# Other start addresses for the operands of both feed-forwards of a two-layer hybrid trunk

## The chip, the cores and the metric

The kernel runs on one core of a Trainium2 chip. The metric is the device time of one launch in microseconds (us), lower is better.

## What is computed

The reference is a trunk of two layers on a sequence of 256 positions with 2048 features, in float32. Layer 0 is differential attention and a gated feed-forward with a causal depthwise convolution (ConvFFN); layer 1 is a gated DeltaNet and another ConvFFN. Each of the four parts works on an RMS-normed copy of x and is added to x. The change touches the two feed-forwards:

```python
def conv_ffn(h, w_up, conv_w, conv_b, w_down):
    u = causal_dwconv(h @ w_up, conv_w) + conv_b
    val, gate = jnp.split(u, 2, axis=-1)
    return (jax.nn.silu(gate) * val) @ w_down

for i in range(DEPTH):
    h = rms_norm(x, mixer_norm[i])
    ...
    x = x + conv_ffn(rms_norm(x, ffn_norm[i]), ffn_w_up[i], ffn_conv_w[i], ffn_conv_b[i], ffn_w_down[i])
```

D_FF is 5504, which is 43 tiles of 128 to each half of w_up.

## The kernel before, in words

Activations lie transposed: features on the 128 partitions, the 256 positions along the free axis. Each float32 operand of a projection is split in two parts, hi (rounded to the type fp32r) and lo (what is left), and a product is made of three matmuls: hi times hi, lo of the weights times hi, hi of the weights times lo (lines 115, 116 and 117). Each matmul loads 128 columns of weights into the array (the stationary operand) and lets 256 columns of activations stream through (the moving operand); in the profile the load is a LDWEIGHTS of its own, on PEld, and overlaps the matmul ahead of it.

Each projection goes through `dense` (line 101), which makes one block of 256 output features: for each chunk of 4 tiles of the contraction, `weights` (line 78) brings the raw weights by a DMA of 512 KB from SyncE's queue, ScalarE casts them to `whi` (line 89), VectorE subtracts to get `wlo` (line 90), and TensorE does 4 x 2 x 3 = 24 matmuls. Raw, whi and wlo have three buffers each. `dense_tok` (line 125) is the other way round: the activations are stationary and the weights moving (line 139); attention's v and DeltaNet's z use it.

A feed-forward (`ffn`, line 251) makes 43 up-blocks (16 contraction tiles each, acts in `h`) with merge, convolution, SiLU and `split` behind each, which leaves one tile row of `ac` (lines 218, 219), and then `project` (line 238) makes 8 down-blocks (43 contraction tiles each, acts in `ac`). When a block of the down-projection has been added to x, the callback `done` writes the next part's normed tiles into `h` (`norm_tile`, lines 152 and 153). Attention's output projection and DeltaNet's do the same for the feed-forward behind them. DeltaNet's output blocks read their acts from tiles `oc`. The order of the work on each engine is the order of the program's lines; small jobs of attention and DeltaNet are fed in between chunks by `tick`.

Where the operands begin is set by hand. Addresses are counted in words of 4 bytes along a partition, modulo 128 words (512 bytes). All rows, chunks and column groups of a tile stand a multiple of 128 words apart, so that one number holds for a whole tile: the first word of `h` is at 40 (HP), of `ac` at 48 (AP; attention's own tiles `ac` too), of `oc` at 112 (OP); the whi and wlo buffers begin at 0 and have 128 words of room, and `weights` puts the block `d` words into them. `dense` takes `d = (place - GAP) % P` with GAP = 45: the weights of every block begin 45 words (180 bytes) ahead of the acts that stream against them. `dense_tok` takes `(HP + GAP) % P` = 85, so that there as well the moving operand stands 45 words behind the stationary one. `rows` cuts a tile of acts in rows that begin `d` words in, and `place(d)` does so for `h`; the kernel before has `d` = 0 in both. `h` and `ac` are allocated with 8 words to spare.

Of the kernel before, what the change touches and what calls it, by code (L numbers as in the profile page):

```python
# [9 lines left out]
F32R = mybir.dt.float32r  # L10
# [6 lines left out]
P = 128  # L17
T = 256
D = 2048
KD = D // P  # L20
EPS = 1e-6
CK = 4
GAP = 45
HP, AP, OP = 40, 48, 112
LNEXP = "natural_log_exp_and_others"

# [1 line left out]
class Trunk:  # L28
# [38 lines left out]
    def mp(self):  # L67
        return self.mps.tile([P, 512], F32, tag="mp", name="mp")
# [29 lines left out]
    def banks(self):  # L98
        return self.dps.tile([P, 2, 2 * T], F32, tag="ps", name="ps")

    def dense(self, w, kt, acts, place, tiles=2, lead=0):

        nc = self.nc
        ps = self.banks()
        for k0, nk in self.chunks(kt, CK, lead):
            hi, lo = self.weights(w[:, k0:k0 + nk, :], (place - GAP) % P)
            steps = [(k, c) for k in range(nk) for c in range(tiles)]
            if k0 + nk == kt:
                steps = [(k, c) for c in range(tiles) for k in range(nk)]
            for k, c in steps:  # L110
                a = acts(k0 + k)
                first, last = k0 + k == 0, k0 + k == kt - 1
                s = slice(c * P, (c + 1) * P)
                o = ps[:, c, :T]
                nc.tensor.matmul(o, hi[:, k, s], a[:, 0, :], start=first, stop=False)  # L115
                nc.tensor.matmul(o, lo[:, k, s], a[:, 0, :], start=False, stop=False)  # L116
                nc.tensor.matmul(o, hi[:, k, s], a[:, 1, :], start=False, stop=last)  # L117
            self.tick()
        return ps
# [5 lines left out]
    def dense_tok(self, w, kt, acts):  # L125
# [3 lines left out]
        for k0, nk in self.chunks(kt, CK // 2):  # L129
            hi, lo = self.weights(w[:, k0:k0 + nk, :], (HP + GAP) % P)  # L130
            for k in range(nk):
# [103 lines left out]
                done(2 * blk + c)  # L235
            self.add_squares()

    def project(self, w, kt, acts, place, done, final=False):

        n = KD // 2  # L240
        for b in range(n):
            ps = self.dense(w[b], kt, acts, place)
            if b < n - final:
                self.add_out(b, ps, done)
                continue
            for c in range(2):
                k = 2 * b + c
                self.nc.vector.tensor_tensor(self.x[:, k, :], ps[:, c, :T], self.x[:, k, :], ALU.add)
                done(k)

    def ffn(self, w_up, w_down, nj, cols_ap, done, final=False):

        nc = self.nc
        self.spawn(self.norm_stat())
        with self.tc.tile_pool(name="fp", bufs=1) as fp:
            cols = fp.tile([P, 8 * nj + 64], F32, tag="fcols", name="fcols")[:, :8 * nj]
            cols = cols.rearrange("p (t h j) -> p t h j", t=4, h=2)
            nc.scalar.dma_start(cols, cols_ap)
            acts = []
            rows = self.rows(fp.tile([P, nj * 2 * T + 8], F32R, tag="ac", name="ac"), nj, 0)  # L260
            for j in range(nj):
                ps = self.dense(w_up[j], KD, self.h_acts, HP)
                c = []
                u = fp.tile([P, 2, T], F32, tag="u", name="u", bufs=2)
                self.merge(ps, u)
                for half in range(2):
                    o = fp.tile([P, T], F32, tag=f"cv{half}", name="cv", bufs=2)
                    c4 = [cols[:, t, half, j:j + 1] for t in range(4)]
                    self.conv(o, u[:, half, :], c4[:3], c4[3])
                    c.append(o)  # L270
                nc.scalar.activation(c[1], c[1], AF.Silu)
                a = c[0]
                nc.vector.tensor_tensor(a, c[0], c[1], ALU.mult)
                ac = rows[j]
                self.split(ac, a)
                acts.append(ac)
            self.project(w_down, nj, lambda k: acts[k], AP, done, final)

    def attention(self, w_qk, w_v, w_o, nh, dist_ap, ident_ap, qg, kg, lvec, sub, start, done, lambda_init):

        nc, mp = self.nc, self.mp
        with self.tc.tile_pool(name="at", bufs=1) as at:
# [27 lines left out]
            def squares(r):  # L310
                sq = at.tile([P, 2, T], F32, tag="sq", name="sq", bufs=2)
                nc.scalar.square(sq, r)
                sp = at.tile([P, 2, 2, T], F32R, tag="sqp", name="sqp", bufs=3)
                self.split(sp, sq)
                return sp
# [51 lines left out]
            def values(h, v, aT):  # L367
                yield
                po = mp()
                for e in range(2):  # L370
                    o = po[:, e * T:(e + 1) * T]
                    es = slice(e * P, (e + 1) * P)
                    nc.tensor.matmul(o, v[:, 0, es], aT[:, :T], start=True, stop=False)
                    nc.tensor.matmul(o[:, P:], v[:, 1, es], aT[:, T:], start=False, stop=True)
                sq = squares(po.rearrange("p (e t) -> p e t", e=2))
                yield
                pn = mp()
                self.total(pn[:, :T], [sq[:, :, e, :] for e in range(2)])
                ri = at.tile([P, 2, T], F32, tag="ri", name="ori", bufs=2)
                self.rsqrt(ri[:, 0, :], pn[:, :T], 2 * P)  # L380
                for e in range(2):
                    on = at.tile([P, T], F32, tag="on", name="on", bufs=2)
                    nc.vector.scalar_tensor_tensor(
                        on, po[:, e * T:(e + 1) * T], subs[:, e:e + 1], ri[:, 0, :], ALU.mult, ALU.mult)
                    ac = at.tile([P, 2, T], F32R, tag=f"ac{h}_{e}", name="ac")
                    self.split(ac, on)
                    outs.append(ac)

            aTs = []
            for h in range(nh):  # L390
                acts, lead = (self.h_acts, 0) if h else (start, 1)
# [6 lines left out]
            for h in range(0, nh, 2):  # L398
                pv = self.dense_tok(w_v[h // 2], KD, self.h_acts)
                v = at.tile([P, 2, 2 * T], F32, tag="v", name="v", bufs=2)  # L400
                for c in range(2):
                    nc.scalar.mul(v[:, c, :], pv[:, c, :], self.rstdc[:, c:c + 1])
                for i in range(2):
                    self.spawn(values(h + i, v[:, :, i * T:(i + 1) * T], aTs[h + i]))
            self.project(w_o, 2 * nh, lambda k: self.await_(outs, k), AP, done)

    def await_(self, items, k):
# [4 lines left out]
    def gdn(self, w_gate, w_in, w_z, w_out, nb, hb, gate_ap, const_ap, hot_ap, conv_col, ng, done):  # L412
# [12 lines left out]
        with tc.tile_pool(name="gd", bufs=1) as gd:  # L425
# [234 lines left out]
                    acts += [oc[:, i] for i in range(2)]  # L660

            def out(b, acts):
                for blk in range(KD // 2):
                    ps = self.dense(w_out[b * (KD // 2) + blk], 2 * hb, lambda k: self.await_(acts, k), OP)
                    self.add_out(blk, ps, done if b == nb - 1 else None)
# [4 lines left out]
            for b in range(nb):  # L670
# [3 lines left out]
                lqs, inv, acts, zts, vts = [], [], [], {}, {}  # L674
                groups = [range(i, i + gh) for i in range(0, hb, gh)]
                plan = [("k", i) for i in range(hb)] + [("v", 0)] + [("z", g) for g in range(len(groups))]
                for op, i in plan + [("v", i) for i in range(1, hb)]:
# [6 lines left out]
                    elif op == "z":  # L684
                        gr = groups[i]
                        zt = zts[i] = gd.tile([P, 2, gv, P], F32, tag="vz", name="zt", bufs=4)
                        ps = self.dense_tok(w_z[heads[gr[0]] // 2], KD, self.h_acts)
# [14 lines left out]
                if pend:  # L702
                    out(*pend)
                pend = (b, acts)
            out(*pend)

    def gates(self, gd, pg, nv, gp, ident, triu, res):
# [133 lines left out]
def trunk_kernel(tc, a, out):  # L841
    nc = tc.nc
    with ExitStack() as ctx:
# [30 lines left out]
        def start(k):  # L874

            if len(begun) <= k:
                if k == 0 or k in starts:
                    load()
                if k == KD - 1:
# [4 lines left out]
            return t.h[k]  # L884

        t.attention(a["w_qk"], a["w_v"], a["w_o"], NH, a["dist"], a["const"][:, :P], qg, kg, lvec, sub, start, then(ffn, 0),
                    0.8 - 0.6 * math.exp(-0.3 * 0))
        t.ffn(a["w_up0"], a["w_down0"], NJ, a["fcols0"], then(mixer, 1))
        t.gdn(a["w_gate"], a["w_in"], a["w_z"], a["w_out"], NB, HB, a["gate"], a["const"], a["hot"],
              lambda tap, tile_: one(gconv, tap * 4 * NQ + tile_), ng, then(ffn, 1))  # L890
        t.ffn(a["w_up1"], a["w_down1"], NJ, a["fcols1"],
              lambda k: nc.sync.dma_start(out[:, k, :], t.x[:, k, :]), final=True)
# [15 lines left out]
```

## Time and profile before

| what | value |
| --- | --- |
| median of the runs | 2675.66 us (2675.52 and 2675.80) |
| the profiled execution, its own time | 2676.33 us |
| its span, first to last instruction | 2674.6 us |
| granted TensorE clock, mean | 0.999 |
| matmuls and weight loads in the trace | 23504 and 23504 |
| first feed-forward, up and down | about 405 to 874 and 874 to 1108 us |
| second feed-forward, up and down | about 1968 to 2437 and 2437 to 2675 us |

A row of a group reads: line, engine, operation, output<-inputs, shapes, xcount | busy us, mean ns of one | idle time of the engine ahead of them and what ended it. A row of a timeline reads: start in us, duration in us, engine, line, operation; neighbours of one kind can be merged into one row with their count. Matmuls overlap in the records, so the pace of TensorE is read from the distance between starts, or from a stretch's length over its count of matmuls, not from the duration of one. In the tables by windows, a count holds a matmul or two that only reach into the window.

### The profile page before, as it was taken

How to read it: one execution, taken by the hardware profiler on the slowest of the kernel's cores; microseconds unless marked ns; L12 is line 12 of the kernel's file. 1: busy time of each engine (PE TensorE's matmuls, PEld its weight loads, DVE VectorE, ACT ScalarE, POOL GpSimd, SP SyncE). 2: the span in 40 equal slices, each digit the busy share in tenths (PEclk: the TensorE clock that was granted, in tenths of full speed). 3: DMA queues.
4: the chain of work that ended last, by engine and by line, in shares of the span. 5: the costliest groups of instructions: out<-in, count | busy, mean ns of one | idle time of the engine just before them, and what ended most of it. 6: DMA issues, size and time to landing. Idle time of an engine off the chain costs nothing.

```text
span 2674.6 us, 55978 instructions
## 1 busy us (share of the span) xinstructions
PE 2656.4 (99%) x23504; PEld 2639.4 (99%) x23504; DVE 1845.2 (69%) x2719; ACT 1453.3 (54%) x1994; POOL 112.1 (4%) x221
## 2 busy tenths in 40 slices
PE   8999999999999999999999999999999999999999
PEld 8999999999999999999999999999999999999999
DVE  7775567777777555688787687688677777776444
ACT  6555555555555444584764664574565555554333
POOL 0000000000000000031011021021000000000000
PEclk9999999999999999999999999999999999999999
DMA  6555566666666666655355454555466666666765
GB/s 205 172 174 164 159 192 194 195 195 193 195 193 195 193 194 192 190 156 177 115 170 166 143 169 155 157 159 174 143 194 195 194 193 196 193 195 197 203 200 165
DMA packets 135469, 481.77 MB, mean 180 GB/s; under 512 B 15408, under 2 KB 18480, under 8 KB 135216
## 3 DMA queue, kind: packets, MB, share of 16 engines
q1 hardware_dynamic: 134064, 475.58, 58.6%
q8 instruction: 184, 3.01, 0.5%
q10 hardware_dynamic: 1152, 2.61, 0.3%
q14 instruction: 69, 0.57, 0.1%
HBM read 476.03 MB, written 2.10 MB: 179 GB/s over the span
## 4 chain that ended last, share of the span: by engine, by line
PE 93%; DVE 3%; ACT 3%; issue 1%; DMA 1%; ACTq 0%; DVEq 0%; SPq 0%
PE ps L115 26%; PE ps L116 26%; PE ps L117 26%; PE ps L139 10%; PE mp L610 2%; DVE wlo L90 1%; ACT whi L89 1%; PE mp L226 1%; DVE cv L207 1%; ACT L455 0%; PE mp L574 0%; PE mp L580 0%; DMA raw<-w_in 0%; PE mp L589 0%; PE mp L498 0%
## 5 line engine op out<-in xcount | busy, mean ns | idle before, releaser
L90 DVE TENSOR_TENSOR wlo<-raw,whi 128x1024 fp32r<-128x1024 f32 (+2 forms) x909 | 1105.2, 1217 | 660.9 <-ACT whi L89 659.8
L89 ACT CAST whi<-raw 128x1024 fp32r<-128x1024 f32 (+2 forms) x909 | 948.6, 1044 | 1034.8 <-PE ps L117 830.8
L115 PE MATMUL ps<-h,whi 128*128 128x256 f32 x4304 | 1195.0, 278 | 7.8 <-ACT h L152 5.6
L116 PE MATMUL ps<-h,wlo 128*128 128x256 f32 x4304 | 1194.8, 278 | 4.4 <-DVE wlo L90 4.4
L117 PE MATMUL ps<-h,whi 128*128 128x256 f32 x4304 | 1193.7, 277 | 0.0
L115 PEld LDWEIGHTS ps<-h,whi 128*128 128x128 f32 x4304 | 809.4, 188 | 9.8 <-ACT h L152 5.6
L116 PEld LDWEIGHTS ps<-h,wlo 128*128 128x128 f32 x4304 | 809.8, 188 | 7.7 <-DVE wlo L90 5.9
L117 PEld LDWEIGHTS ps<-h,whi 128*128 128x128 f32 x4304 | 810.0, 188 | 0.6
L115 PE MATMUL ps<-ac,whi 128*128 128x256 f32 x1632 | 450.4, 276 | 0.0
L116 PE MATMUL ps<-ac,wlo 128*128 128x256 f32 x1632 | 450.3, 276 | 0.0
L117 PE MATMUL ps<-ac,whi 128*128 128x256 f32 x1632 | 450.2, 276 | 0.0
L115 PEld LDWEIGHTS ps<-ac,whi 128*128 128x128 f32 x1632 | 306.2, 188 | 0.0
L116 PEld LDWEIGHTS ps<-ac,wlo 128*128 128x128 f32 x1632 | 306.2, 188 | 0.0
L117 PEld LDWEIGHTS ps<-ac,whi 128*128 128x128 f32 x1632 | 306.2, 188 | 0.0
L139 PE MATMUL ps<-whi,h 128*128 128x256 f32 x1536 | 251.1, 284 | 0.0
L139 PEld LDWEIGHTS ps<-whi,h 128*128 128x128 f32 x1536 | 213.5, 190 | 0.2
L139 PE MATMUL ps<-wlo,h 128*128 128x256 f32 x768 | 155.7, 284 | 1.0 <-DVE wlo L90 1.0
L115 PE MATMUL ps<-oc,whi 128*128 128x256 f32 x512 | 143.9, 281 | 0.0
L207 DVE SCALAR_TENSOR_TENSOR cv<-u,fcols,cv 128x255 f32<-128x255 f32 (+1 forms) x344 | 142.8, 477 | 0.0
L117 PE MATMUL ps<-oc,whi 128*128 128x256 f32 x512 | 142.5, 278 | 0.0
L116 PE MATMUL ps<-oc,wlo 128*128 128x256 f32 x512 | 142.3, 278 | 0.0
L139 PEld LDWEIGHTS ps<-wlo,h 128*128 128x128 f32 x768 | 119.4, 190 | 2.0 <-DVE wlo L90 1.4
(201 smaller groups left out, 2048.7 us busy)
## 6 DMA issues: line engine op xcount, KB each, us to landing
raw<-w_up SPq DMA_DIRECT2D x344, 512.0 KB, 4.3
raw<-w_down SPq DMA_DIRECT2D x160, 512.0 KB, 4.1
raw<-w_in SPq DMA_DIRECT2D x128, 512.0 KB, 4.1
raw<-w_z SPq DMA_DIRECT2D x64, 512.0 KB, 4.4
raw<-w_out SPq DMA_DIRECT2D x64, 512.0 KB, 3.9
raw<-w_qk SPq DMA_DIRECT2D x63, 512.0 KB, 4.0
raw<-w_v SPq DMA_DIRECT2D x32, 512.0 KB, 3.7
raw<-w_o SPq DMA_DIRECT2D x32, 512.0 KB, 4.1
```

What stands on the lines that cost most here:

```text
L89: nc.scalar.copy(hi, raw)
L90: nc.vector.tensor_tensor(lo, raw, hi.bitcast(F32), ALU.subtract)
L115: nc.tensor.matmul(o, hi[:, k, s], a[:, 0, :], start=first, stop=False)
L116: nc.tensor.matmul(o, lo[:, k, s], a[:, 0, :], start=False, stop=False)
L117: nc.tensor.matmul(o, hi[:, k, s], a[:, 1, :], start=False, stop=last)
L139: nc.tensor.matmul(ps[:, c, s], l, r[:, k, s], start=first and not (i or j), stop=last and i + j == 3)
L207: nc.vector.scalar_tensor_tensor(out[:, j:], u[:, :T - j], taps[n - 1 - j], out[:, j:], ALU.mult, ALU.add)
L226: last = self.nc.tensor.matmul(out, self.onesr, p[:, j], start=i + j == 0, stop=i + j == n)
L610: nc.tensor.matmul(p[:, v, :], l(v), r[:, v, :], start=i == 0, stop=i == len(terms) - 1)
```

## The change

The acts of both feed-forwards begin 3 words (12 bytes) later in their tiles: `ac` by `rows(..., ODD)`, `h` by `place(ODD)`, which is called ahead of attention's output projection and ahead of DeltaNet's last output block, so that the normed tiles for the feed-forward are written there. Behind the up-projection of the first feed-forward `place(0)` puts `h` back for DeltaNet.

`dense` gets the distance as an argument. In the up-projections each of the 43 blocks has a distance of its own: 21 to 63 words in the first feed-forward, 64 to 106 in the second (84 to 424 bytes). In the down-projections the 8 blocks have 45, 53, 58, 7, 15, 27, 39 and 3 words in the first, 11, 19, 31, 35, 47, 55, 63 and 0 in the second. The distance is still that from the weights' first word to the acts' first word modulo 128, for whi and wlo alike. Attention, DeltaNet and dense_tok keep 45 and their places.

No instruction, size, buffer or DMA is added or taken away, and on each of the five engines the built programs list the same instructions in the same order; only start addresses of operands differ.

```diff
-GAP = 45
+GAP, ODD = 45, 3
+GAPS = ([*range(21, 64)], [*range(64, 107)])
+PAIRS = ([45, 53, 58, 7, 15, 27, 39, 3], [11, 19, 31, 35, 47, 55, 63, 0])
...
-    def dense(self, w, kt, acts, place, tiles=2, lead=0):
+    def dense(self, w, kt, acts, place, tiles=2, lead=0, gap=GAP):
...
-            hi, lo = self.weights(w[:, k0:k0 + nk, :], (place - GAP) % P)
+            hi, lo = self.weights(w[:, k0:k0 + nk, :], (place - gap) % P)
...
-    def project(self, w, kt, acts, place, done, final=False):
+    def project(self, w, kt, acts, place, done, final=False, gaps=(GAP,) * 8):
...
-            ps = self.dense(w[b], kt, acts, place)
+            ps = self.dense(w[b], kt, acts, place, gap=gaps[b])
...
-            rows = self.rows(fp.tile([P, nj * 2 * T + 8], F32R, tag="ac", name="ac"), nj, 0)
+            rows = self.rows(fp.tile([P, nj * 2 * T + 8], F32R, tag="ac", name="ac"), nj, ODD)
             for j in range(nj):
-                ps = self.dense(w_up[j], KD, self.h_acts, HP)
+                ps = self.dense(w_up[j], KD, self.h_acts, HP + ODD, gap=GAPS[final][j])
...
-            self.project(w_down, nj, lambda k: acts[k], AP, done, final)
+            if not final:
+                self.place(0)
+            self.project(w_down, nj, lambda k: acts[k], AP + ODD, done, final, PAIRS[final])
...
+            self.place(ODD)
             self.project(w_o, 2 * nh, lambda k: self.await_(outs, k), AP, done)
...
             def out(b, acts):
+                if b == nb - 1:
+                    self.place(ODD)
```

## The prediction

> **What bounds the kernel now.** I read the page from the top: the engines' shares, the granted clock, then the chain that ended last.
>
> ```profile
> span 2674.6 us, 55978 instructions
> PE 2656.4 (99%) x23504; PEld 2639.4 (99%) x23504; DVE 1845.2 (69%) x2719; ACT 1453.3 (54%) x1994; POOL 112.1 (4%) x221
> ...
> PEclk9999999999999999999999999999999999999999
> ...
> PE 93%; DVE 3%; ACT 3%; issue 1%; DMA 1%; ACTq 0%; DVEq 0%; SPq 0%
> PE ps L115 26%; PE ps L116 26%; PE ps L117 26%; PE ps L139 10%; PE mp L610 2%; DVE wlo L90 1%; ACT whi L89 1%; PE mp L226 1%; DVE cv L207 1%; ACT L455 0%; PE mp L574 0%; PE mp L580 0%; DMA raw<-w_in 0%; PE mp L589 0%; PE mp L498 0%
> ```
>
> TensorE is busy for 99% of the span at full clock, and the three matmuls of dense are 78% of the chain. Nothing else comes near. So the only thing to ask of an edit is what it does to the spacing from one matmul's start to the next; the 276 to 283 ns that the page gives for one matmul overlap and say little. Next I read that spacing from the table by windows, in stretches where only matmuls of one kind run.
>
> ```profile
> core 0: us, PE busy (x), PEclk, DMA share, GB/s
> 424.00:854.00 430.00, 430.00 (x3796) 1.00 0.64 194
> 874.00:1109.00 235.00, 235.00 (x2076) 1.00 0.65 189
> ```
>
> These are the up-projection of the first feed-forward and its down-projection: 430.00 us over 3796 matmuls is 113.3 ns each, 235.00 over 2076 is 113.2. The timeline shows that this is no average over several speeds: all starts of a piece of it stand 0.11 or 0.12 us apart.
>
> ```profile
> 799.75 0.28 PE L117 MATMUL ps<-h,whi 128*128 128x256 f32 x1
> ...
> 802.92 0.28 PE L115 MATMUL ps<-h,whi 128*128 128x256 f32 x1
> ```
>
> 28 steps in 3.17 us are 113.2 ns. Yet the same three instructions, on tiles that lie at the same distance of 45 words from each other, also run slower, in the DeltaNet layer:
>
> ```profile
> 1432.82 0.28 PE L116 MATMUL ps<-h,wlo 128*128 128x256 f32 x1
> ...
> 1433.66 0.28 PE L117 MATMUL ps<-h,whi 128*128 128x256 f32 x1
> 1433.78 0.28 PE L115 MATMUL ps<-oc,whi 128*128 128x256 f32 x1
> ...
> 1434.13 0.28 PE L115 MATMUL ps<-oc,whi 128*128 128x256 f32 x1
> ...
> 1434.70 0.28 PE L117 MATMUL ps<-oc,whi 128*128 128x256 f32 x1
> ```
>
> From 1432.82 to 1433.78 there are 8 steps in 0.96 us, 120.0 ns each. From 1434.13 to 1434.70 there are 5 in 0.57 us, 114. No engine was waited for in between. What changed is the tile: the weights of the oc block, loaded while h was still streaming, stood for one moment at another distance from the moving rows, and the pace fell to the quick one. An interruption does the same:
>
> ```profile
> 1251.02 0.28 PE L117 MATMUL ps<-h,whi 128*128 128x256 f32 x1
> ...
> 1251.86 0.28 PE L115 MATMUL ps<-h,whi 128*128 128x256 f32 x1
> 1252.07 0.69 PE L553 MATMUL mp<-tcc,lt 32*32 32x32 f32 x32
> ...
> 1253.26 0.28 PE L117 MATMUL ps<-h,whi 128*128 128x256 f32 x1
> ...
> 1255.42 0.28 PE L115 MATMUL ps<-h,whi 128*128 128x256 f32 x1
> ```
>
> Before the 32 small matmuls 7 steps take 0.84 us (120.0), behind them 19 take 2.16 us (113.7). So this stream has two paces, 113.3 and 120.0 ns, both stable for dozens of matmuls, and which one holds depends on how the weight load and the moving stream stand to each other. I take the cause to be that both read SBUF at once and get in each other's way; the rows show the two paces, not the mechanism.
>
> **The change, part by part.** It adds no instruction, removes none and changes no size, and each engine issues the same rows in the same order, SP's and POOL's among them. No wait is added, no DMA is moved. It changes start addresses alone, so there are three things to price.
>
> First, the writers of the moved tiles. dense puts whi and wlo at word 123 or 3 of 128, dense_tok at word 85, and their casts cost, by the groups of 424 to 854 us (dense, first two rows) and of 1207 to 1223 us (dense_tok):
>
> ```profile
> L89 ACT CAST whi<-raw 128x1024 fp32r<-128x1024 f32 x158 | 166.3, 1053 | 187.6 <-PE ps L117 159.5 <-ACT cv L205 25.2 <-DMA raw<-w_up 2.9
> L90 DVE TENSOR_TENSOR wlo<-raw,whi 128x1024 fp32r<-128x1024 f32 x159 | 194.9, 1226 | 107.9 <-ACT whi L89 107.9
> ...
> L89 ACT CAST whi<-raw 128x1024 fp32r<-128x1024 f32 x6 | 6.3, 1051 | 8.0 <-PE ps L139 8.0
> L90 DVE TENSOR_TENSOR wlo<-raw,whi 128x1024 fp32r<-128x1024 f32 x6 | 7.4, 1228 | 1.4 <-ACT whi L89 1.2
> ```
>
> 1053 against 1051 ns and 1226 against 1228: the start makes no difference. Even 100 ns more would lie under the 24 matmuls of a chunk (24 x 113.3 = 2.72 us), since ACT waits for PE there (159.5 us of its idle time). If that cover were gone, 100 ns on each of the 520 chunks (86 blocks of 4, 16 of 11) would cost 52 us; I take nothing. The rows of h and ac begin 12 bytes later; their writers take the same sizes, and I take nothing there either.
>
> Second, the matmuls that read them. They are, from the program, 43 x 16 x 2 x 3 = 4128 in each up-projection and 8 x 43 x 2 x 3 = 2064 in each down-projection, together 12384. The groups of the first feed-forward agree but for a few missing records (1376 and 688 to a line):
>
> ```profile
> L116 PE MATMUL ps<-h,wlo 128*128 128x256 f32 x1366 | 377.1, 276 | 0.0
> ...
> L115 PE MATMUL ps<-ac,whi 128*128 128x256 f32 x688 | 189.9, 276 | 0.0
> ```
>
> Each ns of spacing is therefore worth 12.4 us. No row shows a distance other than 45 in dense, so I bound the price from both sides. From above by dense_tok, the nearest row for a moving tile that begins off the even places (word 85, while h, ac and oc begin at 40, 48 and 112):
>
> ```profile
> 1211.79 0.40 PE L139 MATMUL ps<-wlo,h 128*128 128x256 f32 x2
> 1212.03 0.64 PE L139 MATMUL ps<-whi,h 128*128 128x256 f32 x4
> 1212.51 0.40 PE L139 MATMUL ps<-wlo,h 128*128 128x256 f32 x2
> 1212.75 0.52 PE L139 MATMUL ps<-whi,h 128*128 128x256 f32 x3
> ```
>
> 8 matmuls from 1211.79 to 1212.75, 0.96 us, 120.0 ns: the slow pace again, 6.7 ns over the quick one, 12384 x 6.67 = +83 us. From below by the transposes of L589, which also load 128 columns of weights each (timeline, then the group):
>
> ```profile
> 1192.86 0.60 PE L589 MATMUL mp<-con,cv 128*128 128x128 f32 x4
> ...
> L589 PE MATMUL mp<-con,cv 128*128 128x128 f32 x64 | 9.8, 276 | 0.0
> ```
>
> Four in 0.60 us, the last taking 0.276: (0.60 - 0.276) / 3 is 108 to 109 ns. At 109 the feed-forwards would gain 12384 x 4.3 = 53 us. Between the two ends I lean to the upper: the matmuls of dense never come under 113 in any stretch, while 120 appears both for the off-place start and, at the old distance, after a mere disturbance. And the change disturbs often: every one of its 102 blocks begins with weights at a new distance, where the feed-forwards of before, once quick, were never disturbed. I expect the blocks to divide, and with nothing to tell the shares I take half and half: 6192 x 6.67 = +41 us.
>
> Third, what is not touched: attention's and DeltaNet's matmuls keep their tiles and their distance, so their pace stays. A slower TensorE delays everything behind it alike; the weight DMAs (194 GB/s in the up-projection) would only be asked for less.
>
> The sum: the profiled execution took 2676.33 us, 1.7 beyond its span and 0.7 above the median of the runs, 2675.66. Adding 41 to the median gives **2717 us**.
>
> **The rivals.** (A is the forecast: blocks divide.) B, all slow: the moving tile's start 12 bytes further on costs every matmul what it costs dense_tok, 120.0, so 2676 + 83 = 2758. For it: dense_tok runs at 120.0 at the very distance of 45. Against it: h, at an even place, runs at 120.0 too, so dense_tok may owe its pace to something else. [...]
>
> C, nothing happens: the pace doesn't hang on the distance, and 113.3 stays, 2676. For it: 113.3 holds although successive weights and rows move by 128, 256 and 512 words. Against it: all these are multiples of 128 words, so the distance modulo 128 is 45 throughout and nothing was tried. [...]
>
> D, quicker: some distances let the pair miss each other altogether and the spacing falls toward 109; all of them would give 2676 - 53 = 2623, half of them 2649. For it only the transposes, which are not the same kind of matmul.
>
> E, worse than any row: distances at which the two streams collide more than once, a further step of 6.7 ns to 126.7 for half of the matmuls and 120 for the rest: 123.3 on average, 12384 x 10 = +124, 2800. The point from which this mechanism brings a clear loss is an average of 117.7 ns. For it: the down-projections also go to distances of 0, 3 and 7 words, where both streams begin almost at the same place. Against it: no stretch runs so slowly.
>
> **How the numbers follow.** A 0.42, B 0.25, C 0.17, E 0.10, D 0.06. A measurement of this kernel tells about 2% from no change, 53.5 us, which needs 65% of the feed-forward matmuls at 120. A's own range runs from a quarter to three quarters of them, +21 to +62: 2697 to 2738, with 0.11 of its 0.42 above the line. Slower: 0.11 + 0.25 + 0.10 = 0.46. Faster: the best third of D, 0.02. Within 2%: the rest, 0.52. The range takes in C below and B above with some room, and leaves out D and E: 2672 to 2780.
>
> **What would show it.** Right: the feed-forward windows still hold nothing but back-to-back matmuls at full clock, their spacing steps from block to block between 113.3 and about 120, the two stretches quoted above grow to some 117 ns a matmul, and attention and DeltaNet take their old time. B would show 120 in every block, C 113.3 in every block, D any block under 112, E any over 122. Idle time of PE in front of a wlo or whi would mean that the writers' cover failed, and that the first price was wrong.

## The result, and the profile after

The changed kernel takes 2737.82 us (median of 2737.06 and 2738.59), the kernel before 2675.66: 62 us more, a ratio of 1.0233 with a 95% interval of 1.0212 to 1.0253. The page of the changed kernel, at the places read before (its lines stand two further down, so that L115 to L117 are now L117 to L119, and L139 is L141):

```profile
span 2735.3 us, 55978 instructions
PE 2717.0 (99%) x23504; PEld 2700.2 (99%) x23504; DVE 1852.9 (68%) x2719; ACT 1452.1 (53%) x1994; POOL 112.4 (4%) x221
```

The span is 60.7 us longer and TensorE busy for 60.6 us more; the granted clock is still 0.999. No new wait took the time, as the waits of TensorE show (total, times, longest):

```profile
PE ps L117 <- ACT h L154: 5.6, 1, 5.6
...
PE ps L117 <- ACT whi L91: 2.4, 2, 1.5
```

These are 5.6, 4.4 and 2.4 us, against 5.6, 4.4 and 2.0 for the same three before. The windows that answer to those of the prediction:

```profile
424.00:854.00 430.00, 430.00 (x3631) 1.00 0.60 186
874.00:1109.00 235.00, 235.00 (x1990) 1.00 0.64 186
```

430.00 us hold 3631 matmuls where they held 3796: 118.4 ns each; the second row gives 118.1 (its first 21 us now still belong to the up-projection). Summed over the four feed-forward stretches from the starts in the two traces, 1466.0 us against 1405.3: 60.7, all of the growth of the span. Attention and DeltaNet keep their time (DeltaNet 859.7 us against 860.0).

The pace stands in steps from block to block, and inside a block it is regular. In the timeline, the up-block with 50 words, then the one with 45 words, the distance of before:

```profile
735.79 0.28 PE L119 MATMUL ps<-h,whi 128*128 128x256 f32 x1
...
736.75 0.28 PE L118 MATMUL ps<-h,wlo 128*128 128x256 f32 x1
```

```profile
681.73 0.28 PE L117 MATMUL ps<-h,whi 128*128 128x256 f32 x1
...
683.14 0.28 PE L117 MATMUL ps<-h,whi 128*128 128x256 f32 x1
```

8 steps in 0.96 us are 120.0 ns; 12 in 1.41 us are 117.5 (117.8 over the whole of that block). Over the last two thirds of each of the 102 blocks (pauses left out), 13 run at 116.7 to 117.2 ns, 54 at 117.2 to 118, 13 at 118 to 119.8, and 22 at 119.8 to 120.0. **Not one runs at 113.3.** The same paces come back 64 words further on: 120.0 at 27 and 91, 116.9 at 28 and 92, 118.8 at 29 and 93, 119.9 at 37 and 101.

### The profile page after: what moved, and what is told of

It is laid out like the page before. It is cut to its first block, busy times and chain, and to the rows that moved or that the text cites. A ratio compares the mean times of both kernels' runs of the same rounds, so it can differ in the third digit from the quotient of the medians.

```text
span 2735.3 us, 55978 instructions
## 1 busy us (share of the span) xinstructions
PE 2717.0 (99%) x23504; PEld 2700.2 (99%) x23504; DVE 1852.9 (68%) x2719; ACT 1452.1 (53%) x1994; POOL 112.4 (4%) x221
## 4 chain that ended last, share of the span: by engine, by line
PE 92%; DVE 3%; ACT 3%; DMA 1%; issue 1%; SPq 0%; DVEq 0%; ACTq 0%
PE ps L117 26%; PE ps L119 26%; PE ps L118 26%; PE ps L141 10%; PE mp L615 1%; DVE wlo L92 1%; ACT whi L91 1%; DVE cv L209 1%; DMA raw<-w_in 1%; PE mp L228 1%; ACT L460 0%; PE mp L585 0%; PE mp L579 0%; PE mp L594 0%; PE mp L347 0%
## 5 line engine op out<-in xcount | busy, mean ns | idle before, releaser
L117 PE MATMUL ps<-h,whi 128*128 128x256 f32 x4304 | 1205.3, 280 | 8.0 <-ACT h L154 5.6
L119 PE MATMUL ps<-h,whi 128*128 128x256 f32 x4304 | 1204.8, 280 | 0.0
L117 PEld LDWEIGHTS ps<-h,whi 128*128 128x128 f32 x4304 | 815.6, 190 | 9.9 <-ACT h L154 5.6
L119 PEld LDWEIGHTS ps<-h,whi 128*128 128x128 f32 x4304 | 812.6, 189 | 0.6
L119 PE MATMUL ps<-ac,whi 128*128 128x256 f32 x1632 | 455.9, 280 | 0.0
L117 PE MATMUL ps<-ac,whi 128*128 128x256 f32 x1632 | 455.8, 279 | 0.0
L117 PEld LDWEIGHTS ps<-ac,whi 128*128 128x128 f32 x1632 | 309.2, 189 | 0.0
L119 PEld LDWEIGHTS ps<-ac,whi 128*128 128x128 f32 x1632 | 307.8, 189 | 0.0
L141 PE MATMUL ps<-whi,h 128*128 128x256 f32 x1536 | 251.0, 284 | 0.0
L141 PEld LDWEIGHTS ps<-whi,h 128*128 128x128 f32 x1536 | 213.5, 190 | 0.2
L141 PE MATMUL ps<-wlo,h 128*128 128x256 f32 x768 | 155.8, 284 | 1.0 <-DVE wlo L92 1.0
L117 PE MATMUL ps<-oc,whi 128*128 128x256 f32 x512 | 143.9, 281 | 0.0
L119 PE MATMUL ps<-oc,whi 128*128 128x256 f32 x512 | 142.5, 278 | 0.0
L141 PEld LDWEIGHTS ps<-wlo,h 128*128 128x128 f32 x768 | 119.5, 190 | 1.9 <-DVE wlo L92 1.4
```

The source lines that it names most:

```text
L141: nc.tensor.matmul(ps[:, c, s], l, r[:, k, s], start=first and not (i or j), stop=last and i + j == 3)
```

## The experiments

Eleven kernels were run; a time given without an interval is that of a single run. Paces of single blocks below are worked out like the list above, from the starts in the trace; a window's pace is its length over its count.

**The distances alone.** Starts as before, distances as in the changed kernel:

```diff
-GAP, ODD = 45, 3
+GAP, ODD = 45, 0
```

> The distances of the change alone: the acts of both feed-forwards begin where they began before (h at word 40, ac at 48 of 128), the 86 up-blocks and 16 down-blocks keep the changed kernel's distances. Start theory (the 12 bytes cost, whatever the distance): most blocks are back at 113.3 ns a matmul, the changed kernel's 116.7 to 120 go, and the time is 2676 to 2697 us. Distance theory (the other distances cost, whatever the start): every block keeps the pace that it has in the changed kernel, repeating at 64 words, and the time stays at 2738 us.

Measured 2737.48 us, 1.0229 times before (1.0212 to 1.0246). That is the time of the distance theory, but not its blocks. Four windows of 10 us, inside the blocks with 42, 43, 45 and 37 words:

```profile
647.00:657.00 10.00, 10.00 (x91) 1.00 0.62 193
658.00:668.00 10.00, 10.00 (x85) 1.00 0.58 184
681.00:691.00 10.00, 10.00 (x90) 1.00 0.64 197
590.00:600.00 10.00, 10.00 (x85) 1.00 0.57 188
```

Each count holds two or three that only reach into the window, so 91 and 90 are the quick pace and 85 the slow one. Of 102 blocks seven are quick. The paces of some distances (ns):

| distance in words | starts as before | 12 bytes later |
| --- | --- | --- |
| 22 | 120.0 | 116.9 |
| 27 and 91 | 116.7 | 120.0 |
| 34 and 98 | 119.4 | 116.8 |
| 37 and 101 | 122.2 | 119.9 |
| 42 and 106 | 113.3 | 118.4 |
| 45 | 113.3 | 117.8 |
| 51 | 113.3 | 120.0 |
| 53 | 117.8 | 117.6 to 117.8 |
| 77 (13 + 64) | 113.3 | 117.7 |
| 19, in the down-projection | 113.3 | 117.8 |

The average over all matmuls is 118.4 with the starts as before and 118.3 with them 12 bytes later. So both simple theories fall: a distance that is quick with one start is slow with the other. And 45 and 53 words put the weights equally far from a multiple of 8 words, with the moving tile where it was, yet run at 113.3 and 117.8; and 45 words are quick in the up- and in the down-projection, whose acts begin at words 40 and 48. So it is how the two tiles stand to each other that counts, not only where each begins.

**The start alone.** Every distance 45 words, the acts 12 bytes later:

```diff
-GAPS = ([*range(21, 64)], [*range(64, 107)])
-PAIRS = ([45, 53, 58, 7, 15, 27, 39, 3], [11, 19, 31, 35, 47, 55, 63, 0])
+GAPS = ([45] * 43, [45] * 43)
+PAIRS = ([45] * 8, [45] * 8)
```

> The start of the change alone: h and ac begin 12 bytes later as in the changed kernel, every block has the distance of before, 45 words. Start theory: every feed-forward matmul runs at the 117.8 ns that the two blocks with 45 words show in the changed kernel, 12384 x 4.4 = +55 us, 2731 us. Distance theory: 113.3 ns, 2676 us. Disturbance theory (a block's pace is inherited from the block before it, and 45 words were slow only since their neighbours were): also 113.3 ns and 2676 us, as no neighbour differs.

Measured 2729.94 us, 1.0202 (1.0187 to 1.0217), one us off the start theory's number. All 102 blocks run at 117.8:

```profile
424.00:854.00 430.00, 430.00 (x3653) 1.00 0.59 187
```

430.00 / 3653 is 117.7, and a window of the down-projection (235.00 us, 1997 matmuls) gives the same. No block has a neighbour at another distance here, so the disturbance theory falls as the cause of this loss. Against the kernel before in the same rounds (2676.57 us) the start alone costs 53 us and the distances alone 61, and both together cost 62: they don't add, since the pace of 113.3 is lost only once.

**Other starts.** Distance 45 everywhere, the start by stretch (the diff of the first; the second has 6, 1, 4, 7):

```diff
-GAP, ODD = 45, 3
+GAP, HS, AS = 45, (4, 8), (1, 2)
...
-                ps = self.dense(w_up[j], KD, self.h_acts, HP + ODD, gap=GAPS[final][j])
+                ps = self.dense(w_up[j], KD, self.h_acts, HP + HS[final], gap=GAPS[final][j])
```

> Distance 45 words in every block, four starts: up-projection of the first feed-forward 4 words (16 bytes) later than before, its down-projection 1 word, the second's up-projection 8 words (32 bytes), its down-projection 2 words. Start theory in its simple form (only a whole step of 16 bytes is free): 113.3 ns at 4 and 8, about 117.8 at 1 and 2; the two down-projections then add 4128 x 4.4 = 18 us, 2694 us. If the free step is 32 bytes, the first up-projection is slow as well, +36 us in all, 2712 us. Distance theory: 113.3 everywhere, 2676 us.

> Distance 45 words in every block, four other starts: up-projection of the first feed-forward 6 words later than before, its down-projection 4 words, the second's up-projection 1 word, its down-projection 7 words. Start theory: about 117.8 ns at 6, 1 and 7, and at 4 the same pace as 4 has in the run with starts 4, 1, 8 and 2; with 113.3 there +45 us, 2721 us. Distance theory: 113.3 everywhere, 2676 us.

Measured 2719.17 and 2770.13 us. First up, first down, second up, second down, in the first kernel (starts 4, 1, 8 and 2 words later):

```profile
424.00:854.00 430.00, 430.00 (x3688) 1.00 0.60 188
890.00:1125.00 235.00, 235.00 (x1942) 1.00 0.62 182
2000.00:2430.00 430.00, 430.00 (x3794) 1.00 0.64 194
2470.00:2700.00 230.00, 230.00 (x1917) 1.00 0.66 192
```

That is 116.6, 121.0, 113.3 and 120.0 ns. The other kernel has 121.7 (6), 119.8 (4), 121.1 (1) and 119.9 (7). Of these starts only 8 words, 32 bytes, give the old pace back; 16 bytes do not, and cost 3.3 ns in one stretch and 6.7 in the other. Those two stretches have the same distance and begin at words 44 and 52, exactly 8 words apart, so a step of 8 words does not bring back the pace in every case. Most starts are worse than the 117.8 of the 12 bytes that the change took, and the sizes I had expected, one for all, were too simple.

**Another order.** Starts as before, the up-projections' distances reversed and in the other feed-forward, other distances in the down-projections:

```diff
+GAP, ODD = 45, 0
+GAPS = ([*range(106, 63, -1)], [*range(63, 20, -1)])
+PAIRS = ([19, 51, 13, 42, 45, 61, 62, 49], [13, 51, 19, 42, 45, 29, 12, 4])
```

> Starts as before, the same 86 distances in the up-projections in the opposite order and in the other feed-forward; in the down-projections 19, 51, 13, 42, 45, 61, 62, 49 and 13, 51, 19, 42, 45, 29, 12, 4 words. Address theory: every distance has the pace that it had with even starts before (113.3 at 13, 19, 42, 45 and 51 modulo 64, 115.6 to 122 at the others), in the up-projections the sum is unchanged, and about eight more quick down-blocks take 258 x 5 ns each, 10 us off 2737: 2727 us. Inheritance theory: a distance's pace depends on the block before it, the distances that already showed two paces (19, 22, 28, 29, 32 modulo 64) show others again, and so do many of the rest.

Measured 2725.32 us. Over this run and the one with the distances alone, 53 of the 64 distances (modulo 64 words) repeat their pace within a quarter of a ns whatever stands before them: 37 words 122.2 in all four blocks, 42 113.3 in five, 34 and 98 119.4, 49 119.3 to 119.6. The other eleven have two paces, 0.5 to 6.7 ns apart: 19 runs at 113.3 or 118.2, 13 at 113.3 or 120.0, 48 at 117.8 or 113.3, 29 at 116.7 or 120.0. There something other than the two start addresses decides. The block before is the likely one, but a block's place in the rotation of the buffers changes with the order too, and no run separates the two. So the address theory holds for most distances, and the two paces of the kernel before (45 words at 113.3 and 120.0) are one more such case.

**Fewer weight loads.** One matmul of 512 columns for the two that share whi, in the kernel before and in the changed one:

```diff
-                o = ps[:, c, :T]
-                nc.tensor.matmul(o, hi[:, k, s], a[:, 0, :], start=first, stop=False)
-                nc.tensor.matmul(o, lo[:, k, s], a[:, 0, :], start=False, stop=False)
-                nc.tensor.matmul(o, hi[:, k, s], a[:, 1, :], start=False, stop=last)
+                o = ps[:, c, :]
...
+                nc.tensor.matmul(o, hi[:, k, s], a.rearrange("p i t -> p (i t)"), start=first, stop=last)
...
+                    nc.tensor.matmul(o[:, :T], lo[:, k, s], a[:, 0, :], start=False, stop=False)
```

> The kernel before with the two matmuls that share the whi tile made one of 512 columns (both parts of the acts behind one weight load, the two halves of the result added by one more copy on ScalarE and one more addition on VectorE): two weight loads for three of before. If the 4 ns over the transposes' 109 belong to each weight load, a triple costs 109 + 4 + 2 x 109 + 4 = 335 or less for 340, down to 327 with no conflict left: 6448 triples x 5 to 13 ns, 32 to 84 us off, 2592 to 2644 us. If the pace belongs to the columns streamed, whoever loads: 340 a triple, 2676 us or a little more for the added work.

> The changed kernel (its starts and all its distances) with the same wide matmuls. If the loss is the weight load and the moving stream meeting, it goes with the number of loads and with the cover that a load has: at most two thirds of 62 us over the wide form of the kernel before, 0 to 41 us more than that. [...]

Measured 2754.36 us, 1.0295 (1.0279 to 1.0310), and 2742.75, 1.0253 (1.0236 to 1.0270). Both of my expectations for the first were missed, and that for the second as well: it takes 12 us less than the first, not 0 to 41 more. The first feed-forward's up-projection in the first kernel, then in the second:

```profile
500.00:800.00 300.00, 300.00 (x1729) 1.00 0.62 189
```

```profile
500.00:800.00 300.00, 300.00 (x1727) 1.00 0.63 190
```

Two matmuls make a triple: 300.00 / 864.5 is 347 ns in both. The second feed-forward's up-projection, again in the first kernel and then in the second:

```profile
2100.00:2400.00 300.00, 300.00 (x1704) 1.00 0.61 186
```

```profile
2100.00:2400.00 300.00, 300.00 (x1733) 1.00 0.63 190
```

That is 352 and 346 ns, so the wide form too has two paces at 45 words, and this one stretch makes 8 of the 12 us by which the changed addresses are better. At 45 words a triple got longer with a third of the loads gone (three matmuls of before take 340 ns), at the changed addresses shorter (three matmuls took 3 x 118.3 = 355). A plain price per load would have shortened both. And 45 words, quick for three equal matmuls, are nothing special once the matmuls have another rhythm.

Of the 79 us that the wide form of the kernel before loses, 35 lie in the four feed-forward stretches (1440 us against 1405) and 31 in DeltaNet (891 against 860). There TensorE stands idle for 17 us where it stood for 5, waiting for zt and for small products, 3.7 us at most each; and from about 1900 to 2000 us the granted clock is below full in both wide kernels (0.67 and 0.69 from 1940 to 1960 us, where the kernel before has 1.00). How much of the loss is the clock's was not settled; the feed-forward windows above are at full clock.

**Half loads.** In both feed-forwards the weight load is cut to 64 columns, except for the first and last contraction tile, so that half of the output features lack most of their terms; once with the distances alone and once with the second set of starts:

```diff
-                s = slice(c * P, (c + 1) * P)
-                o = ps[:, c, :T]
+                m = P if first or last else cut
+                s = slice(c * P, c * P + m)
+                o = ps[:m, c, :T]
```

> Starts as before and the changed kernel's distances, but in both feed-forwards all matmuls except those of the first and last contraction tile load 64 columns of weights instead of 128 (half of the output features miss those terms); the moving operand is as it was. Meeting theory (the loss comes from the weight load and the moving stream reading at the same time): a load of half the length meets half as much, the spread between distances shrinks to less than half and the paces fall to 109 to 114 ns, some 11160 matmuls x 4 to 9 ns off 2737, 2637 to 2692 us. Moving theory (the loss is the moving operand's own): every distance keeps its 113.3 to 122 ns, 2737 us.

> Distance 45 words everywhere, starts 6, 4, 1 and 7 words later than before (121.8, 120.0, 121.2 and 120.0 ns with full loads), with the same half loads of 64 columns in the feed-forwards. Meeting theory: the four paces fall to 109 to 115 ns, some 11160 x 6 to 12 ns off 2770, 2636 to 2703 us. [...]

Measured 2723.23 us (distances), between the theories and inside the range of neither, and 2746.88 (starts), above the range of the meeting theory and under the 2770.13 of the same starts with full loads. The loads did become shorter, as the groups of the first kernel from 500 to 800 us show:

```profile
L118 PEld LDWEIGHTS ps<-h,whi 128*64 128x64 f32 x747 | 100.3, 134 | 0.0
...
L118 PEld LDWEIGHTS ps<-h,whi 128*128 128x128 f32 x108 | 20.3, 188 | 0.0
```

134 ns for 188. Yet no block falls under 113.3, the spread is 113.3 to 120.0 (113.3 to 122.2 with full loads), and the average is 117.1 for 118.4 (all paces here without the tiles that keep full loads). What did change is which distances are quick: 0, 16, 22, 33, 36 and 48 words now run at 113.3 beside 42 and 45, where 0 and 22 stood at 120.0 with full loads; 51 fell back to 116.6. With other starts the paces became 119.4, 116.7 and 118.7 by turns from block to block, 120.3 and 117.8, where full loads had 121.8, 120.0, 121.1 and 120.0. Shortening the load moves the paces of a moving operand that was not touched. As the same edit also halves the rows of the result, it does not by itself tell the load from the writing of the result; the run with the distances alone does, since there nothing but the start of the loaded operand differs from the kernel before, and the paces go from 113.3 to 122.2. So the load does have a part in them (against the moving theory). But the loss does not go with the load's length (against the meeting theory as I had put it), and 113.3 is not the length of a full load, since it stays with half of one.

**The other matmul, and a version that beats both kernels.** dense_tok's distance swept, one for each chunk:

```diff
-            hi, lo = self.weights(w[:, k0:k0 + nk, :], (HP + GAP) % P)
+            hi, lo = self.weights(w[:, k0:k0 + nk, :], (HP + self.tok) % P)
+            self.tok += 1
```

> The kernel before with one thing changed: in dense_tok, where the weights are the moving operand and run at 120.0 ns at 45 words, each of the 96 chunks of 24 matmuls has a distance of its own, 0 to 95 words. Address theory (a matmul's pace is set by where the loaded and the moving operand begin, relative to each other and to a step of 32 bytes): paces from about 113 to 122 ns that repeat at 64 words, some chunks at 113.3, 120.0 at 45 again; the mean of about 118 takes some 5 us off, 2671 us. Own-kind theory (dense_tok is slow since it streams two halves against one stationary tile): 120 in every chunk, 2676 us.

Measured 2669.42 us. The last 12 matmuls of each chunk run at 113.3 to 123.3, and again the pace comes back 64 words on (116.7 at 4 and 68, 123.3 at 5 and 69). At 28 and at 92 words, and steadily only there, it is 113.3. The chunk with 28, in the timeline:

```profile
302.77 0.39 PE L141 MATMUL ps<-wlo,h 128*128 128x256 f32 x2
...
304.13 0.39 PE L141 MATMUL ps<-wlo,h 128*128 128x256 f32 x2
```

12 matmuls from 302.77 to 304.13 us, 113.3 ns each, where the kernel before has 120.0. dense_tok's pace was not of its own kind. So it was set to 28 for good, in the kernel before:

```diff
-GAP = 45
+GAP, TOK = 45, 28
...
-            hi, lo = self.weights(w[:, k0:k0 + nk, :], (HP + GAP) % P)
+            hi, lo = self.weights(w[:, k0:k0 + nk, :], (HP + TOK) % P)
```

> The kernel before with dense_tok's distance at 28 words instead of 45, the one distance at which its chunks ran at 113.3 ns (at 28 and at 92, 64 further on). Address theory: its 2304 matmuls go from 120.0 to 113.3, 15 us off, and DeltaNet's dense blocks behind them are less often caught at 120, up to 1056 x 6.7 = 7 us more: 2654 to 2661 us. If the quick pace held only for the one chunk in its place, nothing is gained: 2676 us.

Measured 2657.51 us, 0.9931 times before (0.9917 to 0.9944), 19 us less and the best of all. A window that holds dense_tok alone in both kernels, in the kernel before and then in this one:

```profile
1206.00:1220.00 14.00, 14.00 (x119) 1.00 0.62 196
```

```profile
1206.00:1220.00 14.00, 14.00 (x126) 1.00 0.70 212
```

126 matmuls where the kernel before had 119 in the same 14 us. And dense behind it is caught at 120 less often: intervals of exactly 120 ns between its matmuls go from 1062 to 198. As dense kept its addresses here, this shows that what ran ahead of it decides between its two paces at 45 words.

## Why the prediction was right or wrong, point by point

- **What bounds the kernel** held: TensorE's spacing, at full clock, and nothing else. The change moved 60.7 us of span and 60.6 us of TensorE's busy time.
- **The first price, nothing for the writers,** held: in 424 to 854 us the casts of the changed kernel take 1049 and 1226 ns where they took 1053 and 1226.
- **The count of matmuls** is right, but not its remark on missing records: all 4128 and 2064 of each feed-forward are in the trace. The window of that group began at 413 us, and the up-projection began at 405.
- **The second price, half of the matmuls at 120.0 and half at 113.3,** is the step that failed. I had two paces, because the trace of before shows two, and split the blocks between them. There are many paces, in steps down to a fraction of a nanosecond, and with a start 12 bytes on the quickest of 102 blocks has 116.7. The average came out at 118.3, that is +4.9 ns for 12384 matmuls, +61, where I had +3.3 and +41. What I missed is that 113.3 at 45 words is the exception: with the old starts seven of 102 blocks reach it. A block moved away from such a point runs with the common lot, at about 118; it does not keep 113.3 in half of the cases.
- **Rival B** (the off-place start costs all matmuls 6.7 ns) had the right fact, that the start alone makes every block slower, with too large a size: 4.4 ns at 45 words. Of the other shifts tried there, 16 bytes cost 3.3 and 6.7 ns, and only 32 bytes were free. dense_tok, from which the size came, had a distance of its own to be blamed: at 28 words, again with a start that is no multiple of 8 words, it runs at 113.3.
- **Rival C** (nothing happens) and **D** (quicker) are gone: no block kept 113.3, none came under it. In 102 blocks at two starts, at six other starts and in 96 chunks of dense_tok nothing settled under 113.3. Against C stands the table of distances too: with the starts as before only the loaded operand moves, and the pace goes from 113.3 to 122.2 ns.
- **Rival E** (a further step to 126.7) did not come: 122.2 is the slowest block of any distance at the old starts, 120.0 in the changed kernel, and the distances 0, 3 and 7 run at 120.0, 117.8 and 117.8.
- The range and the sign held. The time lies beyond the 2% that I gave as the line, by a third of a per cent, where I gave 0.52 to within 2% and 0.46 to slower. That it still lies inside my own range for the forecast (to 2738) is luck: the forecast gave 113.3 to at least a quarter of the blocks, and none had it.

What stays open is the mechanism. Shown is that the pace depends on the start addresses of the loaded and of the moving operand: on their distance (113.3 to 122.2 ns with the starts as before), for most of them modulo 64 words, and on their common place (45 words: 113.3, and 117.8 with both tiles 12 bytes later). That this place counts modulo 8 words was seen at one distance and in one stretch, and the 4 words that gave 116.7 and 120.0 speak against it as the whole rule. Shown is also that at 45 words the matmuls ahead decide between two paces, 113.3 and 120.0 (with dense_tok at 28 words the intervals of 120 ns went from 1062 to 198); at eleven other distances that is only likely. That the two streams get in each other's way in SBUF fits this, and that a shorter load changes which distances are quick fits it too, but that was only argued and no run shows it; and why the loss is neither per load nor by the load's length was not settled.

## What to carry to other kernels

When one engine is busy for 99%, read the spacing of its instructions stretch by stretch: two paces for the same instruction on the same shapes can be time to be had (here 120.0 and 113.3 ns in dense_tok, 19 us by one distance). Where matmuls follow each other without a gap, treat the distance between stationary and moving tile as a parameter, here with 64 values, sweep it in one run by giving each block its own, and read the paces from the trace; then keep the start that it was found with, since a quick distance need not be quick at another (45 words: 113.3 ns, and 117.8 with both tiles 12 bytes later). Check every kind of matmul by itself (45 words gave 113.3 in dense and 120.0 in dense_tok), and again when its rhythm changes: another width (at 45 words 347 and 352 ns a triple in the wide form, for 340), another place in the order (19 words: 113.3 or 118.2).

## What the runs showed of the hardware that was not expected

- The pace of an fp32r matmul of 256 columns behind a load of 128 spans 113.3 to 123.3 ns, 9%, by addresses alone, with the same shapes, clock and order (the sweep of dense_tok).
- For most distances (53 of 64, within a quarter of a ns) it repeats when the distance grows by 64 words (256 bytes), and at a distance of 45 words it was the same when both tiles moved by 8 words (32 bytes) together; 1, 2, 3, 4, 6 and 7 words give 116.7 to 121.8 there.
- The quick pace is rare: with the old starts and full loads, 42, 45 and 51 words hold it in every block of the sweeps, 13, 19 and 48 in some, of 64 distances for dense; 28 alone for dense_tok.
- A matmul of 512 columns takes more than two of 256 at a quick distance: in the wide form the next matmul starts 231 ns behind it (two of 256 take 227), and it and the 256 columns of lo take 347 ns together, where three of 256 take 340.
